# Router logits taken from rows that are not normalised yet, with mean and deviation applied to the logits of all tiles at once

## The chip, the cores and the metric

The kernel runs on one core of a Trainium2 chip. The metric is the device time of one execution in microseconds (us); less is better. Five engines work beside each other: TensorE (PE in the profile, with its weight loads as PEld), VectorE (DVE), ScalarE (ACT), GpSimd (POOL) and SyncE (SP), and 16 DMA engines move data for them.

## The reference, cut to what matters

The program is a whole network block followed by a second one of two layers. Each of these two layers is a mixer, a layer norm, and a mixture of 32 experts whose router reads the normalised rows:

```python
h = layer_norm(ALPHA * h + mixed, ln_g[i, 0], ln_b[i, 0])
ffn = hierarchical_moe(h, ...)
h = layer_norm(ALPHA * h + ffn, ln_g[i, 1], ln_b[i, 1])

def layer_norm(x, g, b):
    mu = mean(x); var = mean((x - mu)**2)
    return (x - mu) * rsqrt(var + LN_EPS) * g + b

def hierarchical_moe(h, w_group, b_group, w_expert, b_expert, ...):
    glog = xf @ w_group + b_group        # 4 groups
    elog = xf @ w_expert + b_expert      # 32 experts
    ...                                  # best group, top 2 experts in it, their gates
    ...                                  # each token's row goes through its 2 experts
```

So 36 logits per token (4 and 32) are wanted before any expert can start. Layer 0 has 514 rows here (2 rows of meta tokens and 512 tokens), layer 1 has 512.

## The kernel before, in words

Rows are tiled by 128 tokens: `xt[:, t, :]` holds tile t (128 x 1024, f32), and in layer 0 there is a small tile `hm` of 2 rows ahead of the four. In both layers `mix_ln` (L1812) closes the mixer: `token_mm` (L1496) multiplies the mixer's output by its last weight matrix, in two column halves. The second half is run tile by tile, so that the tiles end one after the other: 24 products of 512 columns each (8 blocks, three products of split operands), written to the bank `pz`.

When a tile's products end, a generator `steps` (L1832) is made for it. Its stages are: (1) `sum_` adds the product to the scaled row and takes the row's sum (DVE, L1830), and `ln_sums` (L1614) makes the negative mean `nm` (DVE) and the sum of squares (ACT, L1622); (2) `ln_norm` (L1626) makes 1/deviation by `rsq` (L345: a square root on ACT, then four small DVE operations and one for `nm`) and normalises the tile in place on ACT (L1629); (3) `xpose` (L2053) turns the tile with 8 PE transposes into two `prt` banks and copies them to `rht`, one half on DVE and one on ACT (L2061); (4) `ln_gain` (L1632) applies gain and bias on DVE and POOL together, for the last tile on DVE alone over all 1024 columns (L1638), and `keep` stores the tile to `dh` in DRAM from POOL's queue (L2041); (5) `route` (L2064) multiplies `rht` by the router's weights `wr` into the bank `plg` (8 products of 36 columns, each two passes in the profile) and adds the bias by a product of one row, `brt` (two passes).

The stages of neighbouring tiles are interleaved by hand in L1527 to L1536: after tile i's products come stage 1 of i, stage 3 of i-1, stage 2 of i, stage 4 of i-1 and stage 5 of i-2. What is left is run after the loop (L1848), and then `logits` (L2076) copies the logits from PSUM to `lg`. These blocks stand in `manual_schedule(engines=VA)`: the order of DVE's and ACT's instructions in such a block is the written one. PE's, POOL's and SP's order is a scheduler's, which takes instructions by the order in which they were written, as far as it holds them for ready.

`fold` (L2043), ahead of the products of `token_mm`, folds the layer norm's gain and bias into the router: `brt` gets bias x `wr` (8 products into `pbr`, an addition on DVE), and `wr` is multiplied by the gain (DVE). `moe` (L2085) starts from `lg`: the first instruction on it is the maximum `gm` (L2114), followed by a chain of small DVE operations, two PE groups (`prk`, `ptab`), a gather of rows (`xg`, POOL's queue) and the first expert's products (`peg`). The experts' weights are streamed from DRAM by SP into a ring of buffers, part of which are filled before `moe` starts.

Of the kernel before, what the change touches and what calls it, by code (L numbers as in the profile page):

```python
# [8 lines left out]
F32 = mybir.dt.float32  # L9
# [3 lines left out]
AF = mybir.ActivationFunctionType  # L13
OP = mybir.AluOpType
# [3 lines left out]
P = 128  # L18
S = 512
D = 1024  # L20
KT = D // P
NT = S // P
# [30 lines left out]
LN_EPS = 1e-5  # L53
# [9 lines left out]
VA = {mybir.EngineType.DVE, mybir.EngineType.Activation}  # L63
# [1432 lines left out]
def token_mm(e, nk, xx, done, tiles, before_tail=None, tail=8, steps=False):  # L1496

    left = deque()
    st = e.st
    for h in range(2):
        pz = [e.bank(f"pz{t}") for t in range(len(tiles))]

        def part(w, k, i):
            tk = tiles[i]
            e.mm3(pz[i][:tk.stop - tk.start], (xx[0][k][:, tk], xx[1][k][:, tk]), (w[0], w[1]), k == 0, k == nk - 1)

        k = 0
        while k < (nk if h == 0 else nk - tail):
            w = st.get()
            for i in range(len(tiles)):
                for j in range(w[0].shape[1]):
                    part([x[:, j, :] for x in w], k + j, i)
                if h == 0 and k + w[0].shape[1] == nk:
                    done(i, 0, pz[i])
            k += w[0].shape[1]
        if h == 1:  # L1520
            if before_tail:
                before_tail()
            ww = [st.get() for _ in range(tail // 2)]
            for i in range(len(tiles)):
                for j in range(tail):
                    part([x[:, j % 2, :] for x in ww[j // 2]], nk - tail + j, i)
                if steps:  # L1527
                    new = done(i, 1, pz[i])
                    last = list(left)[-1:]
                    with e.tc.manual_schedule(engines=VA):  # L1530
                        for g in [new] + last + [new] + last:
                            next(g)
                        if len(left) > 1:
                            next(left.popleft(), None)
                    left.append(new)
                    continue  # L1536
                if len(left) >= 2:
                    left.popleft()()
                left.append(done(i, 1, pz[i]))
    return left  # L1540
# [73 lines left out]
def ln_sums(e, pool, h, n, sums, junk, tag=""):  # L1614

    nm = pool.tile([P, 1], F32, name="lnm" + tag, bufs=4)[:n]
    ss = pool.tile([P, 1], F32, name="lns" + tag, bufs=4)[:n]
    if len(sums) == 2:
        e.ts(nm, sums[0], sums[1], -1.0 / D, OP.add, OP.mult)
    else:  # L1620
        e.ts(nm, sums[0], -1.0 / D)
    e.A.activation(junk, h, AF.Square, bias=nm, accum_out=ss)  # L1622
    return nm, ss


def ln_norm(e, pool, h, n, nm, ss, tag=""):  # L1626
    r = e.rsq(pool, ss, n, LN_EPS, "lnr" + tag)
    e.mul(nm, nm, r)
    e.A.activation(h, h, AF.Identity, scale=r, bias=nm)  # L1629


def ln_gain(e, h, n, g, b, c):  # L1632

    c = D - c
    for x, op in ((g, OP.mult), (b, OP.add)):
        if c < D:
            e.G.tensor_tensor(h[:, c:], h[:, c:], x[:n, c:], op=op)  # L1637
        e.V.tensor_tensor(h[:, :c], h[:, :c], x[:n, :c], op=op)  # L1638
# [173 lines left out]
def mix_ln(e, sp, zz, tiles, hs, mo):  # L1812


    e.st.limit = e.mark2 if mo.l else e.mark
    g = e.brow(sp, "ln_g_2", D, off=(mo.l * 2) * D, tag="lng0")
    b = e.brow(sp, "ln_b_2", D, off=(mo.l * 2) * D, tag="lnb0")
    sums = {}
    mo.fold()

    def done(i, h, p_):
        if h:
            return steps(i, p_)
        sum_(i, h, p_)

    def sum_(i, h, p_):
        n = tiles[i].stop - tiles[i].start
        c = slice(h * 512, h * 512 + 512)
        s_ = sums[i, h] = sp.tile([P, 1], F32, name=f"sum{i}{h}")[:n]
        e.V.scalar_tensor_tensor(hs[i][:, c], hs[i][:, c], ALPHA, p_[:n], op0=OP.mult, op1=OP.add, accum_out=s_)  # L1830

    def steps(i, p_):  # L1832
        sum_(i, 1, p_)
        n = tiles[i].stop - tiles[i].start
        nm, ss = ln_sums(e, sp, hs[i], n, [sums[i, 0], sums[i, 1]], sp.tile([P, D], BF, name="lnj")[:n])
        yield
        ln_norm(e, sp, hs[i], n, nm, ss)
        yield
        ht = mo.xpose(sp, hs[i], n)
        yield  # L1840
        t = i - (len(tiles) - NT)
        t = NT if t < 0 else t
        ln_gain(e, hs[i], n, g, b, 0 if i == len(tiles) - 1 else 448)
        mo.keep(t, hs[i], n)
        yield
        mo.route(ht, t, n)

    left = token_mm(e, KT, zz, done, tiles, steps=True)  # L1848
    with e.tc.manual_schedule(engines=VA):
        for gen in left:  # L1850
            for _ in gen:
                pass
        mo.logits()
# [41 lines left out]
def shortconv(e):  # L1895
# [62 lines left out]
    with tc.tile_pool(name="lo", bufs=1, reuse_waits="tile") as op:  # L1958
        mix_ln(e, op, z, [slice(t * P, (t + 1) * P) for t in range(NT)], [xt[:, t, :] for t in range(NT)], e.mo)
# [3 lines left out]
class Moe:  # L1963
# [76 lines left out]

        self.e.G.dma_start(self.dh[t * P:t * P + n, :], h)  # L2041

    def fold(self):  # L2043

        e = self.e
        pg, pb = [e.pc((n, 2 * D) if self.l else n, 0, KT) for n in ("ln_g_2", "ln_b_2")]
        pt = e.bank("pbr")[0:1, :36]
        for k in range(KT):
            e.mm(pt, pb[:, k:k + 1], self.wr[:, k, :], k == 0, k == KT - 1)
        e.add(self.br, self.br, pt)  # L2050
        e.mul(self.wr, self.wr, pg.unsqueeze(2).to_broadcast([P, KT, 36]))

    def xpose(self, pool, h, n):  # L2053

        e = self.e
        ht = pool.tile([P, KT, P], F32, name="rht", bufs=2)
        for k0 in (0, 4):
            pt = e.bank("prt")
            for k in range(4):
                e.tr(pt[:, k * P:k * P + n], h[:, (k0 + k) * P:(k0 + k + 1) * P])  # L2060
            (e.A.copy if k0 else e.V.tensor_copy)(ht[:, k0:k0 + 4, :n], pt.rearrange("p (k t) -> p k t", k=4)[:, :, :n])  # L2061
        return ht

    def route(self, ht, t, n):  # L2064

        e = self.e
        if self.pl is None:
            self.pl = e.bank("plg"), (e.bank("plg") if self.nt > NT else None)
        pl = self.pl[0][:, t * 36:(t + 1) * 36] if t < NT else self.pl[1][:n, :36]
        for k in range(KT):  # L2070
            e.mm(pl, ht[:, k, :n], self.wr[:, k, :], k == 0, False)
        e.mm(pl, self.one[:, :n], self.br[0:1, :], False, True)
        if t == NT:
            e.A.copy(self.lg[:n, t, :], pl)

    def logits(self):  # L2076

        self.done = self.e.A.copy(self.lg[:, :NT, :].rearrange("p t c -> p (t c)"), self.pl[0][:, :NT * 36])

    def run(self):  # L2080
        moe(self.e, self)
# [500 lines left out]
```

## Time and profile before

| | us |
|---|---|
| median of 3 runs (2554.54 to 2555.36) | 2554.92 |
| the profiled execution | 2554.61 |
| its span in the profile | 2552.8 |
| PE busy | 2300.2 (90%) |
| DVE busy | 944.4 (37%) |
| ACT busy | 666.8 (26%) |

The page's row of 40 slices shows PE at seven tenths or more nearly all the time; the DMA engines are nearly full in two stretches, slices 21 to 28 and 33 to 39, which are the experts of layer 0 and layer 1 (about 1278 to 1750 us and 2025 to 2510 us). Ahead of each stand the end of the mixer and the router. The busy time of an engine over the whole span says little about a change that sits in two stretches of some 90 us; the timelines of these stretches do. A row of a timeline has the start and the duration in us, engine, line, operation, what it writes and reads, the number of merged instructions, and in brackets the idle time before it with what ended it.

### The profile page before, as it was taken

The page shows a single profiled execution, that of the slowest core. Times are in us where ns is not written, and L with a number is a line of the kernel's source. Part 1 is how long each engine was busy: PE and PEld are TensorE (multiplying, and loading weights), DVE is VectorE, ACT ScalarE, POOL GpSimd, SP SyncE. Part 2 cuts the span into 40 slices and gives each one's busy share as a digit, 9 for nine tenths or more (in the row PEclk, how much of TensorE's full clock was granted, in tenths as well). Part 3 has the DMA queues.
Part 4 walks back from the last instruction along what each step waited for, and adds up shares of the span by engine and source line. Part 5 has one row for each costly group of instructions (what it writes and reads, how often), then busy time and mean ns, then how long its engine had stood idle before and what let it go on. Part 6 is the DMA issues. An engine that isn't in the chain of part 4 may idle for free. (4 is left out here: it accounts for less than half of the span.)

```text
span 2552.8 us, 37528 instructions
## 1 busy us (share of the span) xinstructions
PE 2300.2 (90%) x15343; PEld 1470.3 (58%) x15343; DVE 944.4 (37%) x2162; ACT 666.8 (26%) x1058; POOL 226.5 (9%) x264
## 2 busy tenths in 40 slices
PE   7998999999999999999799899884899798899881
PEld 6886777877888888887632233221798532233220
DVE  4348868765533332565620000003644610000003
ACT  4335432123422322375300000013322210000012
POOL 0023120000100000100200000001200210000002
PEclk9999999999999999999799999997899799999996
DMA  4221221025133242224589999998225599999993
GB/s 142 91 80 43 87 70 63 23 79 187 53 106 92 90 140 91 80 82 147 221 342 418 419 415 416 412 415 313 61 87 227 224 399 418 419 413 414 415 405 122
DMA packets 176434, 556.87 MB, mean 218 GB/s; under 512 B 22248, under 2 KB 104934, under 8 KB 127106
## 3 DMA queue, kind: packets, MB, share of 16 engines
q1 hardware_dynamic: 154308, 523.29, 53.0%
q0 software_dynamic: 12768, 25.31, 2.7%
q10 hardware_dynamic: 9184, 5.84, 0.8%
q8 instruction: 122, 2.00, 0.3%
q14 instruction: 52, 0.43, 0.1%
HBM read 548.02 MB, written 25.21 MB: 225 GB/s over the span
## 5 line engine op out<-in xcount | busy, mean ns | idle before, releaser
L300 PE MATMUL peg<-sr,ext 128*32 128x512 f32 (+1 forms) x4064 | 527.6, 599 | 70.9 <-DMA sr<-in_moe_w_gate_dram 38.7
L300 PEld LDWEIGHTS peg<-sr,ext 128*32 128x32 f32 (+1 forms) x4064 | 142.4, 111 | 410.8 <-issue 276.7
L300 PE MATMUL pey<-sr,eh 128*32 128x512 f32 x1984 | 303.3, 597 | 14.1 <-DMA sr<-in_moe_w_down_dram 11.8
L300 PEld LDWEIGHTS pey<-sr,eh 128*32 128x32 f32 x1984 | 82.0, 110 | 193.5 <-issue 148.6
L227 DVE TENSOR_TENSOR sh_0l<-sr,sh_0h 128x1024 fp32r<-128x1024 f32 x84 | 103.5, 1232 | 163.4 <-ACT sh_0h L225 162.8
L285 DVE TENSOR_TENSOR eh<-eh,peg 128x512 f32<-128x512 f32 x34 | 23.4, 688 | 367.4 <-PE peg L300 367.4
L2321 ACT COPY eys<-pey 128x512 f32<-128x512 f32 x68 | 39.9, 586 | 428.9 <-PE pey L300 428.4
L225 ACT CAST sh_0h<-sr 128x1024 fp32r<-128x1024 f32 x84 | 88.1, 1049 | 238.4 <-PE pf L300 53.2
L2264 DVE COPY ext<-pex 128x512 f32<-128x512 f32 x32 | 22.0, 689 | 311.1 <-PE pex L319 311.1
L227 DVE TENSOR_TENSOR sh_1l<-sr,sh_1h 128x1024 fp32r<-128x1024 f32 (+1 forms) x65 | 77.4, 1191 | 107.0 <-ACT sh_1h L225 106.7
L227 DVE TENSOR_TENSOR sh_2l<-sr,sh_2h 128x1024 fp32r<-128x1024 f32 (+1 forms) x65 | 74.2, 1141 | 94.5 <-ACT sh_2h L225 94.2
L225 ACT CAST sh_1h<-sr 128x1024 fp32r<-128x1024 f32 (+1 forms) x65 | 66.5, 1022 | 147.3 <-PE pf L300 48.5
L225 ACT CAST sh_2h<-sr 128x1024 fp32r<-128x1024 f32 (+1 forms) x65 | 62.9, 967 | 151.8 <-PE pf L300 49.3
L2290 ACT ACTIVATE eh<-peg 128x512 f32<-128x512 f32 x34 | 20.3, 597 | 278.0 <-PE peg L300 278.0
L300 PE MATMUL pl<-hlo,sh_0h 128*128 128x264 f32 (+3 forms) x288 | 87.5, 304 | 2.2 <-DVE hlo L309 2.2
L300 PE MATMUL pl<-hhi,sh_0h 128*128 128x264 f32 (+3 forms) x288 | 87.8, 305 | 0.8 <-ACT hhi L308 0.8
L300 PE MATMUL pl<-hhi,sh_0l 128*128 128x264 f32 (+3 forms) x288 | 87.0, 302 | 0.0
L2322 POOL DMA_INDIRECT dy<-eys,yix x34 | 33.9, 998 | 576.2 <-ACT eys L2321 559.8
L2300 DVE COPY eh<-pex 128x512 f32<-128x512 f32 x34 | 23.3, 691 | 136.0 <-PE pex L319 136.0
L2178 POOL DMA_INDIRECT xg<-dh,tix x34 | 35.4, 1041 | 326.3 <-PE pex L319 244.7
L2264 ACT COPY ext<-pex 128x512 f32<-128x512 f32 x36 | 21.1, 586 | 163.2 <-PE pex L319 118.7
L300 PEld LDWEIGHTS pl<-hlo,sh_0h 128*128 128x128 f32 x288 | 56.2, 195 | 5.0 <-DVE hlo L309 3.2
(747 smaller groups left out, 4898.2 us busy)
## 6 DMA issues: line engine op xcount, KB each, us to landing
sr<-in_moe_w_gate_dram SPq DMA_DIRECT2D x128, 1024.0 KB
sr<-in_moe_w_up_dram SPq DMA_DIRECT2D x122, 1024.0 KB
sr<-in_moe_w_down_dram SPq DMA_DIRECT2D x122, 1024.0 KB
sr<-in_w_in_dram SPq DMA_DIRECT2D x34, 1024.0 KB
sr<-in_sc_w_in_dram SPq DMA_DIRECT2D x12, 1024.0 KB
sr<-in_ffn_w_gate_dram SPq DMA_DIRECT2D x11, 1024.0 KB
sr<-in_ffn_w_up_dram SPq DMA_DIRECT2D x11, 1024.0 KB
sr<-in_ffn_w_down_dram SPq DMA_DIRECT2D x10, 1024.0 KB
```

The costliest lines, as they stand in the source:

```text
L225: self.e.A.copy(hi, r)
L227: v.tensor_tensor(lo, r, f(hi), op=OP.subtract)
L285: V.tensor_tensor(out_, a, b, op=OP.mult)
L300: T.matmul(o, l, r, start=start, stop=stop)
L2178: G.indirect_dma_start(out=xg[i], out_offset=None, in_=dh[:, :], in_offset=bass.IndirectOffsetOnAxis(ap=ti, axis=0), bounds_check=n_tok - ...
L2264: (A.copy if k0 or first else V.tensor_copy)(x_[:, k0:k0 + 4, :].rearrange("p k c -> p (k c)"), pt)
L2290: A.activation(sg, pg, AF.Silu)
L2300: V.tensor_copy(hh.rearrange("p k c -> p (k c)"), pt)
L2321: e.late = A.copy(ys[:, h * 512:(h + 1) * 512], po[h])
L2322: G.indirect_dma_start(out=dy[:, :], out_offset=bass.IndirectOffsetOnAxis(ap=yi, axis=0), in_=ys, in_offset=None, bounds_check=2 * n_tok - ...
```

## The change

`mean` and `deviation` are no longer applied to the rows ahead of the router. The turned tile holds the rows before normalisation, and the logits follow from L = r (x wr + nm c) + b, with c the column sums of the folded `wr` and b the folded bias. `fold` computes c for all 128 partitions by 8 products with a tile of ones, brings b to all partitions by one more product, and copies both to `cb`. `scales` keeps `nm` and r of each tile in `mr`. `route` loses the bias product, and for the 2-row tile its copy. `logits` does four DVE operations per group of tiles (the four full tiles; in layer 0 also the 2-row tile) in place of the ACT copy. The stages become three: (1) sums, r and the two copies to `mr`; (2) turning the tile, then normalising, gain, bias and store; (3) `route`. Stage 2 of a tile is issued in the middle of the next tile's products, stage 3 after them.

```diff
--- before.py
+++ after.py
@@ -1498,7 +1498,6 @@
 
 
 
-
     left = deque()
     st = e.st
     for h in range(2):
@@ -1524,15 +1523,15 @@
             for i in range(len(tiles)):
                 for j in range(tail):
                     part([x[:, j % 2, :] for x in ww[j // 2]], nk - tail + j, i)
+                    if steps and left and j == tail // 2 - 1:
+                        with e.tc.manual_schedule(engines=VA):
+                            next(left[0])
                 if steps:
-                    new = done(i, 1, pz[i])
-                    last = list(left)[-1:]
+                    left.append(done(i, 1, pz[i]))
                     with e.tc.manual_schedule(engines=VA):
-                        for g in [new] + last + [new] + last:
-                            next(g)
+                        next(left[-1])
                         if len(left) > 1:
                             next(left.popleft(), None)
-                    left.append(new)
                     continue
                 if len(left) >= 2:
                     left.popleft()()
@@ -1816,7 +1815,7 @@
     g = e.brow(sp, "ln_g_2", D, off=(mo.l * 2) * D, tag="lng0")
     b = e.brow(sp, "ln_b_2", D, off=(mo.l * 2) * D, tag="lnb0")
     sums = {}
-    mo.fold()
+    mo.fold(sp)
 
     def done(i, h, p_):
         if h:
@@ -1832,14 +1831,15 @@
     def steps(i, p_):
         sum_(i, 1, p_)
         n = tiles[i].stop - tiles[i].start
+        t = i - (len(tiles) - NT)
+        t = NT if t < 0 else t
         nm, ss = ln_sums(e, sp, hs[i], n, [sums[i, 0], sums[i, 1]], sp.tile([P, D], BF, name="lnj")[:n])
-        yield
-        ln_norm(e, sp, hs[i], n, nm, ss)
+        r = e.rsq(sp, ss, n, LN_EPS, "lnr")
+        mo.scales(t, n, nm, r)
         yield
         ht = mo.xpose(sp, hs[i], n)
-        yield
-        t = i - (len(tiles) - NT)
-        t = NT if t < 0 else t
+        e.mul(nm, nm, r)
+        e.A.activation(hs[i], hs[i], AF.Identity, scale=r, bias=nm)
         ln_gain(e, hs[i], n, g, b, 0 if i == len(tiles) - 1 else 448)
         mo.keep(t, hs[i], n)
         yield
@@ -2040,15 +2040,29 @@
 
         self.e.G.dma_start(self.dh[t * P:t * P + n, :], h)
 
-    def fold(self):
+    def fold(self, pool):
 
         e = self.e
+        ones, self.cb, self.mr = [pool.tile([P] + sh, F32, name=n) for n, sh in
+                                  (("rone", [P]), ("rcb", [72]), ("rmr", [2, self.nt]))]
+        e.V.memset(ones, 1.0)
         pg, pb = [e.pc((n, 2 * D) if self.l else n, 0, KT) for n in ("ln_g_2", "ln_b_2")]
-        pt = e.bank("pbr")[0:1, :36]
+        pt = e.bank("pbr")
         for k in range(KT):
-            e.mm(pt, pb[:, k:k + 1], self.wr[:, k, :], k == 0, k == KT - 1)
-        e.add(self.br, self.br, pt)
+            e.mm(pt[0:1, :36], pb[:, k:k + 1], self.wr[:, k, :], k == 0, k == KT - 1)
+        e.add(self.br, self.br, pt[0:1, :36])
         e.mul(self.wr, self.wr, pg.unsqueeze(2).to_broadcast([P, KT, 36]))
+
+        pt = e.bank("pbr")
+        for k in range(KT):
+            e.mm(pt[:, :36], ones, self.wr[:, k, :], k == 0, k == KT - 1)
+        e.mm(pt[:, 36:72], self.one, self.br, True, True)
+        e.V.tensor_copy(self.cb, pt[:, :72])
+
+    def scales(self, t, n, nm, r):
+
+        self.e.V.tensor_copy(self.mr[:n, 0, t:t + 1], nm)
+        self.e.V.tensor_copy(self.mr[:n, 1, t:t + 1], r)
 
     def xpose(self, pool, h, n):
 
@@ -2068,14 +2082,21 @@
             self.pl = e.bank("plg"), (e.bank("plg") if self.nt > NT else None)
         pl = self.pl[0][:, t * 36:(t + 1) * 36] if t < NT else self.pl[1][:n, :36]
         for k in range(KT):
-            e.mm(pl, ht[:, k, :n], self.wr[:, k, :], k == 0, False)
-        e.mm(pl, self.one[:, :n], self.br[0:1, :], False, True)
-        if t == NT:
-            e.A.copy(self.lg[:n, t, :], pl)
+            e.mm(pl, ht[:, k, :n], self.wr[:, k, :], k == 0, k == KT - 1)
 
     def logits(self):
 
-        self.done = self.e.A.copy(self.lg[:, :NT, :].rearrange("p t c -> p (t c)"), self.pl[0][:, :NT * 36])
+        e = self.e
+        for t0, t1, n, pl in ((0, NT, P, self.pl[0]), (NT, self.nt, 2, self.pl[1])):
+            if t0 < t1:
+                sh = [n, t1 - t0, 36]
+                lg = self.lg[:n, t0:t1, :]
+                of = lambda k: self.mr[:n, k, t0:t1].unsqueeze(2).to_broadcast(sh)
+                row = lambda k: self.cb[:n, k * 36:(k + 1) * 36].unsqueeze(1).to_broadcast(sh)
+                e.V.tensor_tensor(lg, row(0), of(0), op=OP.mult)
+                e.add(lg, lg, pl[:n, :(t1 - t0) * 36].rearrange("p (t c) -> p t c", c=36))
+                e.V.tensor_tensor(lg, lg, of(1), op=OP.mult)
+                e.V.tensor_tensor(lg, lg, row(1), op=OP.add)
 
     def run(self):
         moe(self.e, self)
```

## Rows read from the trace of the kernel before

**Rows 1.** Busy time by stretch: stretch, length, engines with instruction counts, PE clock, DMA share, GB/s

```profile
1184.00:1245.50 61.50, 61.50 (x303) 45.12 (x301) 29.89 (x72) 23.27 (x35) 8.63 (x9) 1.00 0.51 197
1268.00:1272.00 4.00, 1.73 (x9) 1.65 (x8) 3.36 (x6) 0.00 (x0) 0.00 (x0) 0.50 0.00 0
1944.00:1992.80 48.80, 48.80 (x244) 40.49 (x244) 20.28 (x50) 14.86 (x20) 5.81 (x6) 1.00 0.60 228
```

**Rows 2.** Timeline of PE, layer 1, between the third and the fourth tile

```profile
1984.16 1.03 PE L319 MATMUL prt<-ident,xt 128*128 128x128 f32 x8
1985.03 1.87 PE L300 MATMUL plg<-wr,rht 128*128 128x36 f32 x16
1986.84 0.41 PE L300 MATMUL plg<-brt,stage 1*128 1x36 f32 x2
1987.17 0.50 PE L300 MATMUL pz<-sh_0h,zh 128*128 128x512 f32 x1
1987.51 0.40 PE L300 MATMUL pz<-sh_0l,zh 128*128 128x512 f32 x1
```

**Rows 3.** Timeline of PE, layer 1, after the last tile's products

```profile
1992.78 1.04 PE L319 MATMUL prt<-ident,xt 128*128 128x128 f32 x8
1993.65 1.87 PE L300 MATMUL plg<-wr,rht 128*128 128x36 f32 x16
...
1998.23 1.97 PE L319 MATMUL prt<-ident,xt 128*128 128x128 f32 x8
2000.13 3.63 PE L300 MATMUL plg<-wr,rht 128*128 128x36 f32 x16
```

**Rows 4.** Timeline of DVE, layer 1, from the last tile's sum to the router

```profile
1992.98 0.69 DVE L1830 SCALAR_TENSOR_TENSOR xt<-xt,pz 128x512 f32<-128x512 f32 x1 [3.22 <-PE pz L300]
...
1996.82 0.75 DVE L1638 TENSOR_TENSOR xt<-xt,lng 128x576 f32<-128x576 f32 x1
...
1999.38 0.69 DVE L2061 COPY rht<-prt 128x512 f32<-128x512 f32 x1 [1.02 <-PE prt L319]
2000.31 1.23 DVE L1638 TENSOR_TENSOR xt<-xt,lng 128x1024 f32<-128x1024 f32 x1 [0.23 <-PE prt L319]
2004.75 0.17 DVE L2114 TENSOR_REDUCE gm<-lg 128x4 f32<-128x16 f32 x1 [1.96 <-ACT lg L2078]
```

**Rows 5.** Timeline of ACT, layer 1, the last tile's normalisation

```profile
1996.94 1.24 ACT L1629 ACTIVATE xt<-xt,lnm,lnrr 128x1024 f32<-128x1024 f32 x1 [1.07 <-DVE lnm L285]
```

**Rows 6.** Timeline of DVE, layer 0, the 2-row tile from its sum to r

```profile
1217.66 0.68 DVE L1830 SCALAR_TENSOR_TENSOR hm<-hm,pz 2x512 f32<-2x512 f32 x1 [3.23 <-PE pz L300]
...
1220.82 0.15 DVE L285 TENSOR_TENSOR lnrr<-lnrr,lnrt 2x1 f32<-2x1 f32 x1
```

**Rows 7.** Timeline of DVE, layer 1, one operation of the router and the next

```profile
2006.32 0.29 DVE L285 TENSOR_TENSOR sel<-lg,ge 128x128 f32<-128x128 f32 x1
2006.65 0.38 DVE L2130 TENSOR_REDUCE el<-sel 128x32 f32<-128x128 f32 x1
```

**Rows 8.** Timeline of PE and of DVE, layer 0: last products' end, router's start

```profile
1245.53 1.03 PE L319 MATMUL prt<-ident,xt 128*128 128x128 f32 x8
...
1257.51 0.18 DVE L2114 TENSOR_REDUCE gm<-lg 128x5 f32<-128x20 f32 x1 [1.94 <-ACT lg L2078]
```

**Rows 9.** Timeline of all engines around `fold`, layer 0

```profile
1183.10 0.62 ACT L1771 ACTIVATE lm<-lav 128x528 f32<-128x528 f32 x1
...
1183.40 0.68 PE L300 MATMUL pbr<-wr,par 128*1 128x36 f32 x16
...
1184.12 0.18 DVE L288 TENSOR_TENSOR brt<-brt,pbr 1x36 f32<-1x36 f32 x1 [1.75 <-PE pbr L300]
1184.22 0.44 DVE L285 TENSOR_TENSOR wr<-wr,par 128x288 f32<-128x288 f32 x1
...
1184.60 0.69 DVE L297 SCALAR_TENSOR_TENSOR lm<-lm,ltg 128x528 f32<-128x528 f32 x1
```

**Rows 10.** Timeline of ACT, layer 0, the loads into the pool of `mix_ln`

```profile
1195.87 0.37 ACTq L397 DMA_DIRECT2D lng<-in_ln_g_dram  x1
```

## The prediction

> **What bounds the kernel now.** I read the 40 slices of the page first, then busy time by stretch, then the timelines of PE, DVE and ACT in the two stretches that the change touches, and last the timeline of all engines around `fold`. The page's chain of waits covers only the end of the execution, so it says nothing here. From the start of the last mixer product to the end of it PE is busy without a gap, 61.5 of 61.5 us in layer 0 and 48.8 of 48.8 us in layer 1, at the full clock of 2.4 GHz [rows 1]. Any PE instruction added there moves the end of the products by its own pace. After the products, PE's part ends and a chain of one tile decides: sum, r, normalise (ACT), turn (PE), copy, logits (PE), copy, `gm`. From the end of the last products to `gm` it is 2004.75 - 1992.78 = 11.97 us in layer 1 and 1257.51 - 1245.53 = 11.98 us in layer 0 [rows 3, 4, 8]. The DMA engines have by then filled all the buffers they may: in layer 0 they move 0 GB/s just before the experts begin, and the page's slices show them full from then to the end of the experts. So the experts' stream starts when the router lets it, and a microsecond won or lost before `gm` is one at the end, in each layer. What is to be worked out is therefore where `gm` starts in each layer.
>
> **Prices.** PE at full clock, from start to start [rows 2]: 8 transposes 1985.03 - 1984.16 = 0.87; the 16 passes of one tile's logits 1.81; the bias product 0.33; and the first dense product after such a group takes 0.34 instead of 0.23 (the other 23 of the tile need 1992.78 - 1987.51 = 5.27), so each return costs 0.11 [rows 2, 3]. On DVE an operation on 128 x 128 elements is followed by a dependent one after 0.33 [rows 7], and one on 1 x 36 elements takes 0.18 [rows 9].
>
> **Part 1, `fold`.** It adds 8 products of 36 columns with a full 128 x 128 weight tile, the form of one tile's logits (1.81), one product with a single row (0.33), and one return (0.11): 2.25 us of PE per layer. The products need the scaled `wr`, which DVE ends at 1184.66 [rows 9], when PE is already in its dense stretch; there is no gap that could hide them [rows 1]. So 2.25 is on the path; the upper end is 0.7 more, if PE meets them right behind `pbr` and waits for `wr`, the lower end is 1.1, if the 16 passes cost no more than the 16 of `pbr`, 0.68 [rows 9], which have the same 36 columns but a weight tile of one column. I take 2.25, since the trace has the very form in the logits. The memset of ones and the copy to `cb` are one small DVE operation each beside PE's work, where DVE is busy 29.9 of 61.5 us [rows 1]; were they late, only the products of `fold` would feel it (rival 3).
>
> **Part 2, the order on PE.** Before, the turn of tile 2, the logits of tile 1 and, behind them, those of tile 2 ran after the last dense product, under the chain of the last tile, whose own turn begins at 1998.23 [rows 3]: hidden. Now the turn of tile 2 stands in the middle of the last tile's products, and the logits of tile 1 stand ahead of them. Only the logits of tile 2 are left for the shelter. So the last product ends later by 0.87 + 1.81. Three more returns cost 0.33, one bias product (that of tile 0) is gone, -0.33: 2.68 in layer 1. In layer 0 there is the 2-row tile too: four more returns, two bias products gone of which the small one is about 0.2: 0.87 + 1.81 + 0.44 - 0.53 = 2.59. With `fold` the products end 4.93 us later in layer 1 and 4.84 in layer 0. The SP queue's loads into the split buffers wait for these products and slide along, but they end several us before they are wanted [rows 1].
>
> **Part 3, the chain of the last tile.** Let E be the end of its products on PE. The sum starts at E + 0.2 if DVE is free [rows 3, 4]. It isn't: tile 2's turn ends about E - 2.8 (half a tile's products and a return later PE is at E); then come the copies of `rht` (0.69 on DVE, about 0.6 on ACT), the normalisation on ACT (1.24, to E - 0.8) and gain and bias on DVE, 2 x 0.79, and all of this is written ahead of the last tile's sum. So the sum starts at about E + 0.7. If it could pass them it would be E + 0.2; that is the lower end. From the sum to r it is 1220.97 - 1217.66 = 3.3 in a tile where nothing stands between [rows 6]: E + 4.0. Then in DVE's order: the two copies to `mr` 0.25; the copy of `rht` 0.65 (the turn, freed at E + 1.8 by the logits of tile 2, is long done); `nm` x r 0.17; ACT's normalisation 1.24 and 0.12 for the two hand-overs [rows 5]; gain and bias over all 1024 columns, 2.45 [rows 4]; and only then the four operations of `logits` on 144 elements, 4 x 0.32 [rows 7]. `gm` starts at E + 0.7 + 3.3 + 0.25 + 0.65 + 0.17 + 1.36 + 2.45 + 1.28 = E + 10.2. Layer 0 has four more operations on the 2-row tile, 4 x 0.2: E + 11.0. PE doesn't bind: its last 16 passes start when `rht` is copied, E + 4.9, and at the low clock of 1.2 GHz, at which the trace shows them (3.6 [rows 3]), end at E + 8.6, before DVE asks for them at E + 9.2. What the change saves here is the normalisation and the turn ahead of the logits; what it puts in their place is the same normalisation, with gain and bias, ahead of the four operations, because they stand in one DVE queue.
>
> That a DVE instruction holds up what is behind it shows once in the trace: the addition to `brt` waits 1.75 us for PE, and the next-but-one instruction, whose input from ACT was there at 1183.72, starts at 1184.60 [rows 9]. The Trainium skill says the same more broadly (TensorE: Matmul & The Clock Gate, on the architecture of the array): the queues of ScalarE and VectorE are strictly first in, first out, and only TensorE's may pull weight loads forward. That rule speaks against this change as it is written; without it rival 1 would be the likelier, at 2553.7 instead of 2561.7 for the execution, and the one wait in the trace agrees with the rule.
>
> **Sum.** Layer 1: 4.93 + 10.2 - 11.97 = +3.2. Layer 0: 4.84 + 11.0 - 11.98 = +3.9. Together +7.1 on the profiled execution of 2554.61 us; the median of the runs is 0.3 higher, so I say 2562.0. With the lower ends (sum not held up, `fold` at 1.1) it is 7.1 - 1.0 - 2.3 = +3.8; with the upper one of `fold` +8.5. POOL's store of the last tile slides with gain and bias to about E + 9, its memsets behind it to E + 12; the gather follows `gm` by 13 us and more (it did in the trace of before) and doesn't see it.
>
> **Rivals.**
> 1. The change does what it says: DVE takes the copy of `rht` while ACT squares, and the four operations don't stand behind the normalisation. Then `rht` is there at E + 3.3, the logits at full clock end at E + 5.1, r at E + 3.5, and `gm` starts at E + 6.2 (layer 0: 7.0). Layer 1: 4.93 + 6.2 - 11.97 = -0.8; layer 0: 4.84 + 7.0 - 11.98 = -0.1. That is 2554.0 on the median's scale: not slower. Even so it gains next to nothing, since the shelter of part 2 is paid for. For it speaks that the data would allow it; against it the written order of DVE and ACT. It decides if DVE's operations of the last tile appear out of the written order.
> 2. The same chain, but shorter on one side: the scheduler lets the last tile's sum pass tile 2's gain and bias (they stand in different blocks), or leaves the turn of tile 2 behind the last products. Some 1 to 4 us less than the forecast: +3 to +5, 2558 to 2560.
> 3. `fold` stalls PE. The tile of ones lies in a pool whose first loads are only issued at 1195.87 in layer 0, when the memory of the stage before is given up [rows 10]. If PE's order has the products of `fold` early, at 1184, PE waits up to 11 us there, and the time is 2566 to 2573. Against it: in the trace DVE waited for PE at `fold` and not PE for DVE [rows 9], so PE is rather late against the order it was given.
> 4. A gain of over 5 us: needs the products of `fold` and the turn of tile 2 both off the path, for which I see no place.
>
> **How the numbers follow.** The forecast (+5 to +10) has 0.52, rival 1 0.16 (-3 to +2), rival 2 0.18, rival 3 0.08, rival 4 0.06. What a measurement of this kernel can tell from no change is about 0.2%, 5.1 us. The edge of that bound, 2560.0, lies at the foot of the forecast's range, so a part of it (0.04) counts as no change: slower 0.48 + 0.08 = 0.56; same 0.16 + 0.18 + 0.04 = 0.38; faster 0.06. The range from 2553.5 to 2567 leaves out rival 4, the low half of rival 1 and most of rival 3.
>
> **What would show it.** In the profile of the changed kernel: 16 passes of `wr` with ones and two of one row, some 2.2 us of PE, near 1184 and 1944, without an idle PE; the last `pz` group of layer 1 ending near 1997.7 and of layer 0 near 1250.4; tile 2's turn in the middle of the last group; the last tile's sum on DVE right behind the second `lnb` operation of tile 2; the 1024-column gain and bias ahead of the four operations; `gm` near 1261.4 in layer 0 and, shifted by layer 0's 3.9, near 2011.8 in layer 1; the experts' stretches as long as before. It is wrong if the four operations come ahead of the gain, if the dense stretches end less than 4 us later, or if a stretch of the experts changes its length by more than the two stretches before it.

## The result, and the profile after

The changed kernel is slower: 2583.21 us (median of 4 runs, 2581.49 to 2585.37) against 2554.73 us (2554.34 to 2555.36) for the kernel before, a ratio of 1.0112 with a 95% interval of 1.0098 to 1.0127. That is 28.5 us more, where 7.1 had been forecast, and outside the range of 2553.5 to 2567. The span of the profiled execution is 2579.8 us against 2552.8. `gm` starts 20.55 us later in layer 0 (1278.06) and 27.76 later in layer 1 (2032.51) [rows 4, 8]. So some 20 us are lost ahead of `gm` of layer 0 and some 7 more ahead of that of layer 1; from there to the end nothing is lost (547.3 us against 548.0).

The first view is busy time by stretch of the changed kernel (columns as in [rows 1]; the first and third stretch hold `fold`, the others the dense products behind it).

```profile
1182.60:1201.00 18.40, 5.13 (x37) 4.62 (x36) 8.95 (x15) 8.34 (x13) 0.00 (x0) 0.64 0.30 96
1201.00:1266.20 65.20, 65.20 (x322) 48.06 (x320) 25.80 (x71) 17.03 (x24) 12.41 (x10) 0.97 0.44 168
1963.80:1969.50 5.70, 3.09 (x36) 2.79 (x35) 3.04 (x6) 1.56 (x2) 0.00 (x0) 0.98 0.87 309
1969.50:2021.30 51.80, 51.80 (x250) 43.34 (x250) 21.04 (x55) 14.10 (x19) 8.55 (x7) 0.97 0.51 185
```

PE, which had no gap in [rows 1], is busy for 5.13 of 18.40 us and for 3.09 of 5.70 us. Its timeline says what it waited for (such a time in which PE is idle is called a stand below); layer 0 around `fold`, then layer 1:

```profile
1182.66 0.68 PE L300 MATMUL pbr<-wr,par 128*1 128x36 f32 x16
1196.61 3.60 PE L300 MATMUL pbr<-wr,rone 128*128 128x36 f32 x16 [13.27 <-DVE rone L2048]
...
1200.71 0.59 PE L300 MATMUL pz<-sh_0h,zh 128*2 128x512 f32 x1
...
1204.08 0.63 PE L300 MATMUL pz<-sh_0h,zl 128*128 128x512 f32 x1
1204.51 0.49 PE L300 MATMUL pz<-sh_0h,zh 128*128 128x512 f32 x1
```

```profile
1963.87 0.68 PE L300 MATMUL pbr<-wr,par 128*1 128x36 f32 x16
1967.16 1.95 PE L300 MATMUL pbr<-wr,rone 128*128 128x36 f32 x16 [2.61 <-DVE rone L2048]
...
1969.40 0.79 PE L300 MATMUL pz<-sh_0h,zh 128*128 128x512 f32 x1
1970.00 0.63 PE L300 MATMUL pz<-sh_0l,zh 128*128 128x512 f32 x1
```

Before each group of 16 passes with `rone`, the tile of ones, PE stands for 13.27 and 2.61 us until DVE's memset of it is done. Afterwards it runs at half pace: dense products follow each other by 0.43 us instead of 0.23, from 1200.71 to 1204.8 in layer 0 and from 1969.40 to 1972.8 in layer 1. The granted clock is 0.51 in both stretches (the level of 1.2 GHz) and 1.00 (2.4 GHz) right behind them. DVE shows the other side, layer 0, then layer 1:

```profile
1193.66 1.27 DVE L285 TENSOR_TENSOR lgx<-lm,yb 128x514 f32<-128x514 f32 x2
1195.02 1.30 DVE L309 TENSOR_TENSOR zl<-lgx,zh 128x514 fp32r<-128x514 f32 x2
1196.30 0.17 DVE L2048 MEMSET rone<- 128x128 f32 x1
```

```profile
1965.07 1.21 DVE L227 TENSOR_TENSOR sh_0l<-sr,sh_0h 128x1024 fp32r<-128x1024 f32 x1
1966.20 0.67 DVE L309 TENSOR_TENSOR zl<-szc,zh 128x512 fp32r<-128x512 f32 x1
1966.85 0.17 DVE L2048 MEMSET rone<- 128x128 f32 x1
```

The memset is 0.17 us long, and it stands behind the last operations of the mixer. The program's own tile addresses say why it can't be earlier in layer 0: `rone` occupies bytes 81280 to 81792 of each partition, and the two buffers of `yb` of the stage before 77184 to 81408 and 81408 to 85632, so that it overlaps both; the last reading of `yb`, from the second, is the first line above, over at 1194.93. In layer 1 (80544 to 81056) the memory is free by 1917.7, as e2 below shows in its trace; there the memset only stands behind the operations of the mixer that are queued ahead of it, the last two of which take from 1965.07 to 1966.85.

The tail of layer 1 on DVE, and the same time on POOL:

```profile
2020.43 0.76 DVE L1637 TENSOR_TENSOR xt<-xt,lng 128x576 f32<-128x576 f32 x1 [1.44 <-ACT xt L1842]
2021.23 1.58 DVE L1637 TENSOR_TENSOR xt<-xt,lnb 128x576 f32<-128x576 f32 x1
2022.73 0.67 DVE L1829 SCALAR_TENSOR_TENSOR xt<-xt,pz 128x512 f32<-128x512 f32 x1
...
2028.61 1.22 DVE L1637 TENSOR_TENSOR xt<-xt,lng 128x1024 f32<-128x1024 f32 x1 [1.31 <-ACT xt L1842]
2029.87 1.22 DVE L1637 TENSOR_TENSOR xt<-xt,lnb 128x1024 f32<-128x1024 f32 x1
2031.01 0.30 DVE L2096 TENSOR_TENSOR lg<-rcb,rmr 128x144 f32<-128x144 f32 x1
...
2032.51 0.17 DVE L2135 TENSOR_REDUCE gm<-lg 128x4 f32<-128x16 f32 x1
...
2032.65 1.28 DVE L2393 CAST eh<-pid 128x128 f32<-128x128 int32 x1
2032.79 1.15 DVE L2137 TENSOR_TENSOR ge<-lg,gm 128x16 f32<-128x16 f32 x1
```

```profile
2020.48 1.70 POOL L1636 TENSOR_TENSOR xt<-xt,lng 128x448 f32<-128x448 f32 x1 [3.95 <-ACT xt L1842]
2022.26 1.54 POOL L1636 TENSOR_TENSOR xt<-xt,lnb 128x448 f32<-128x448 f32 x1
...
2031.93 1.86 POOL L2122 MEMSET xg<- 128x1024 f32 x2
```

The order is the one forecast: the last tile's sum right behind tile 2's second `lnb` operation, and the 1024-column gain and bias ahead of the four operations that make the logits. Two durations are not: the second operation of tile 2 takes 1.58 us, and the first operations behind `gm` 1.15 to 1.28.

### The profile page after: what moved, and what is told of

Same layout as the page of the kernel before. It is cut to its first block, busy times and chain, and to the rows that moved or that the text cites. A ratio compares the mean times of both kernels' runs of the same rounds, so it can differ in the third digit from the quotient of the medians.

```text
span 2579.8 us, 37602 instructions
## 1 busy us (share of the span) xinstructions
PE 2297.9 (89%) x15361; PEld 1468.4 (57%) x15361; DVE 954.2 (37%) x2196; ACT 666.0 (26%) x1055; POOL 232.9 (9%) x264
```

## The experiments

Each kernel is timed beside the kernel before on its own chip (2554.25 to 2554.76 us). To see past the differences of a few us with which the stretches begin, the table takes two lengths from each profile: A, from the start of `pbr` at `fold` to the start of the last dense product, and B, from there to `gm`. e2, e3, e9 and e11 have their numbers in their own parts.

| kernel | median, us | ratio to before (95%) | A, layers 0 / 1 | B, layers 0 / 1 | A + B of both, against before |
|---|---|---|---|---|---|
| before | 2554.3 to 2554.8 | | 61.90 / 48.47 | 12.21 / 12.20 | |
| after | 2583.21 | 1.0112 (1.0098 to 1.0127) | 83.22 / 57.13 | 12.18 / 11.51 | +29.3 |
| e1, ones early | 2563.52 | 1.0036 (1.0021 to 1.0050) | 66.97 / 53.70 | 12.18 / 11.52 | +9.6 |
| e5, e1 and logits first | 2562.43 | 1.0031 (1.0020 to 1.0041) | 66.97 / 53.72 | 12.01 / 11.32 | +9.2 |
| e7, e1 and turns as before | 2564.27 | 1.0033 (1.0021 to 1.0046) | 64.29 / 51.03 | 15.72 / 14.55 | +10.8 |
| e4, cheap fold | 2561.75 | 1.0025 (1.0015 to 1.0035) | 65.09 / 51.80 | 12.18 / 11.52 | +5.8 |
| e8, e4 and normalising beside logits | 2555.87 | 1.0005 (0.9996 to 1.0015) | 65.09 / 51.81 | 10.34 / 9.75 | +2.2 |
| e10, e8 and two operations | 2554.96 | 1.0000 (0.9990 to 1.0009) | 65.08 / 51.82 | 9.97 / 9.41 | +1.5 |
| e12, e10, gain on POOL, memory moved | 2555.91 | 1.0006 (0.9997 to 1.0015) | 65.09 / 51.82 | 7.30 / 6.23 | -4.3 |

**e1: the ones made early.** They go into a constant of the router, written when each layer begins (1065.7 and 1808.6) and refilled with its own numbers after `fold`.

```diff
-        G.iota(const("slot", [P]), pattern=[[1, P]], ...)
+        V.memset(const("slot", [P]), 1.0)
...
-        e.V.memset(ones, 1.0)
+        ones = self.slot
...
         e.V.tensor_copy(self.cb, pt[:, :72])
+        e.G.iota(ones, pattern=[[1, P]], ...)
```

> The changed kernel, but the tile of ones is not set in fold: it is the router's own constant tile, filled with ones when the layer begins and given its final content after fold; all of the 18 products of fold stay, and only what they wait for is gone. Theory (PE stands at fold because the memset of ones runs late on VectorE, 13.3 us in layer 0 and 2.6 us in layer 1, and the dense products after the pause run their first microseconds at 1.2 GHz): the two stalls and most of the slow products go, 2583.2 - 21 = 2562, between 2560 and 2564. Rival (the loss sits in the new order on PE and in the last tile's chain): no change, 2581 to 2584.

Measured 2563.52 us: 19.7 of the 28.5 us are gone. PE at `fold` in layer 0:

```profile
1183.45 0.68 PE L300 MATMUL pbr<-wr,par 128*1 128x36 f32 x16
1184.87 1.95 PE L300 MATMUL pbr<-wr,slot 128*128 128x36 f32 x16 [0.73 <-ACT ltg L1764]
...
1187.08 0.39 PE L300 MATMUL pz<-sh_0h,zh 128*2 128x512 f32 x1
```

The stand is 0.73 us and no slow stretch follows (granted clock 1.00 from 1187.08 on). The row names ACT for it; the scaled `wr`, which the passes read, is done at 1184.72, and layer 1 of e2 names it. By the table A loses 16.25 us in layer 0 and 3.43 in layer 1, 19.7 as the medians say. Of the 16.25, 14.4 are the longer stretch from `pbr` to the first dense product (18.05 against 3.63); the rest is the lower clock behind it.

**e2: the memset on GpSimd** (`e.G.memset(ones, 1.0)`), which takes it out of DVE's queue and leaves it in its memory.

> The changed kernel, but the memset of ones is issued on GpSimd, into the same tile at the same place. If the memset is late because of what stands ahead of it in VectorE's queue, GpSimd does it at once and the time is that of the run with the ones set early, about 2562. If it is late because its memory is still held by the stage before, the pause in layer 0 stays (11 to 13 us) and the one of layer 1 goes or not with its memory: 2575 to 2583.

Measured 2577.39 us, ratio 1.0093 (1.0076 to 1.0110). The timeline of PE, layer 0, then layer 1:

```profile
1196.80 3.63 PE L300 MATMUL pbr<-wr,rone 128*128 128x36 f32 x16 [11.98 <-POOL rone L2048]
...
1963.91 1.95 PE L300 MATMUL pbr<-wr,rone 128*128 128x36 f32 x16 [0.73 <-DVE wr L285]
```

DVE and POOL in layer 0:

```profile
1195.16 1.27 DVE L285 TENSOR_TENSOR lgx<-lm,yb 128x514 f32<-128x514 f32 x2
1196.54 0.21 POOL L2048 MEMSET rone<- 128x128 f32 x1 [131.56 <-ACT zh L308]
```

Layer 0 keeps a stand of 11.98 us, with POOL idle ahead of the memset: it waits for the memory, and starts at 1196.54, right behind the last reading of `yb`, over at 1196.43. (The row names ACT for the wait; the program has the memset wait for that reading.) A of layer 0 is 81.43 us, 1.79 less than in the changed kernel. In layer 1 the memset starts at 1917.7, early, and only the 0.73 us of `wr` remain: there it was the place in DVE's queue.

**e3: the added part of `fold` alone**, in the kernel before; nobody reads what it makes.

```diff
+        ones, self.cb, self.mr = [pool.tile([P] + sh, F32, name=n) for n, sh in ...]
+        e.V.memset(ones, 1.0)
...
+        for k in range(KT):
+            e.mm(pt[:, :36], ones, self.wr[:, k, :], k == 0, k == KT - 1)
+        e.mm(pt[:, 36:72], self.one, self.br, True, True)
+        e.V.tensor_copy(self.cb, pt[:, :72])
```

> The kernel before with only the added part of fold (the tile of ones, the 9 products, the copy), whose results nobody reads; logits, stages and order are those of before. Theory: fold alone carries most of the loss: 2 x 2.25 us for the products and 21 for the pauses and the clock after them, 2554.7 + 25.5 = 2580, between 2576 and 2584. Rival (the loss sits in the order and the chain): only the products' own 4.5, 2559.

Measured 2580.24 us, ratio 1.0099 (1.0082 to 1.0116); PE stands 13.27 us ahead of the products again. `fold` alone costs 25.9 us (against 2554.33), nearly all of the 28.5.

**e5: the last tile's logits written ahead of its normalisation, gain and store**, on top of e1.

```diff
         ht = mo.xpose(sp, hs[i], n)
+        if i == len(tiles) - 1:
+            mo.route(ht, t, n)
+            yield
         e.mul(nm, nm, r)
...
-        for gen in left:
-            for _ in gen:
-                pass
+        next(left[0])
         mo.logits()
+        for _ in left[0]:
+            pass
```

> The run with the ones set early, and for the last tile of a layer the logits written ahead of its normalisation, gain, bias and store. Theory (in VectorE's queue the normalisation, 1.2 us on ScalarE with its hand-overs, and 2.5 us of gain and bias stand between r and the four operations): 3.9 us less per layer than with the ones set early alone, 2562 - 7.8 = 2554, that is, about as fast as the kernel before. Rival (something else, as PE's last products, holds the logits): less than 2 us in all, 2560 or more.

Measured 2562.43 us, not 2554. The logits did come first, and `gm` didn't follow them. DVE in layer 1:

```profile
2011.49 0.31 DVE L2103 TENSOR_TENSOR lg<-lg,rcb 128x144 f32<-128x144 f32 x1
...
2013.18 1.23 DVE L1637 TENSOR_TENSOR xt<-xt,lng 128x1024 f32<-128x1024 f32 x1 [1.31 <-ACT xt L1845]
2014.44 1.23 DVE L1637 TENSOR_TENSOR xt<-xt,lnb 128x1024 f32<-128x1024 f32 x1
2015.58 0.16 DVE L2139 TENSOR_REDUCE gm<-lg 128x4 f32<-128x16 f32 x1
```

The wait for ACT's normalisation and the two gains only changed places with the four operations: `gm`, the router's first instruction, still has them ahead of it in DVE's queue.

**e7: the turns as before**, the turn of a tile after the next tile's products and its logits one tile later, on top of e1.

```diff
-                    if steps and left and j == tail // 2 - 1:
-                        with e.tc.manual_schedule(engines=VA):
-                            next(left[0])
                 if steps:
+                    last = list(left)[-1:]
                     left.append(done(i, 1, pz[i]))
                     with e.tc.manual_schedule(engines=VA):
-                        next(left[-1])
-                        if len(left) > 1:
+                        for x in [left[-1]] + last:
+                            next(x)
+                        if len(left) > 2:
                             next(left.popleft(), None)
```

> The changed kernel with the ones taken early (2563.5), but the tiles' turns and logits again interleaved as before the change: the turn of the next-to-last tile after the last tile's products, its logits after that, instead of both ahead of the last products. Theory that PE's order sets the end of the stage (Part 2 of the prediction): the last products end 2.6 to 2.7 us earlier in each layer, 2558. Rival that VectorE's chain from the last sum to gm sets it: the earlier end of the products only puts the copies of two turns and the gain of the tile before between the last sum and gm, and the time stays at 2562 to 2564; gm then comes 2 to 3 us later after the end of the last products than the 11 to 12 us of the changed kernel.

Both halves can be read. The dense products do end earlier by 2.68 us in each layer (A), the 0.87 + 1.81 of the prediction's part 2. B grows by 3.54 and 3.03, since the turn, normalisation and gain of tile 2 then stand between the last sum and `gm`. 2564.27 us: nothing is won, and the chain on DVE decides.

**e4: column sums with a weight of one column.** In `fold` the raw `wr` is multiplied by the gain column instead of the scaled `wr` by ones, and one product with a row of ones spreads the result after the first tile's first half.

```diff
-        e.V.memset(ones, 1.0)
...
-            e.mm(pt[0:1, :36], pb[:, k:k + 1], self.wr[:, k, :], k == 0, k == KT - 1)
+        for c, x in ((0, pg), (36, pb)):
+            for k in range(KT):
+                e.mm(pt[0:1, c:c + 36], x[:, k:k + 1], self.wr[:, k, :], k == 0, k == KT - 1)
...
-            e.mm(pt[:, :36], ones, self.wr[:, k, :], k == 0, k == KT - 1)
+    def spread(self):
+        pt = self.e.bank("pbr")
+        self.e.mm(pt[:, :72], self.one, self.rw, True, True)
```

> The column sums that fold needs are taken with the gain column as a weight of one column (16 passes, like the 16 of the added bias) instead of with a 128x128 tile of ones, and are spread over the partitions by one small product after the last products of the first tile. No tile of ones, so no wait of PE for it. Theory (what is left after the pause is the sum of the prediction, of which fold is 2.25 us of PE per layer): 16 products of 128*1 cost 0.68 us a layer where the 16 of 128*128 cost 1.95, so 1.2 to 1.3 us a layer less than in the kernel with the ones taken early (2563.5): about 2561. Rival (the rest of the loss lies in the last tile's chain on VectorE alone, and PE's products at fold are covered): no change, 2563.5. Rival (the slower clock after a short stand costs more than the products): PE's idle time of 0.7 us at fold stays and the time is 2563 to 2564.

Measured 2561.75 us. A falls by 1.88 and 1.90 us, more than the 1.2 to 1.3 expected, since the stand of 0.73 us for `wr` is gone too:

```profile
1184.73 1.20 PE L300 MATMUL pbr<-wr,par 128*1 128x36 f32 x32
1185.86 0.39 PE L300 MATMUL pz<-sh_0h,zh 128*2 128x512 f32 x1
```

**e8: the last tile in one block**, on top of e4: its turn's copies behind the square, its logits ahead of gain and store, so that ACT normalises while DVE makes the logits.

```diff
+        end = i == len(tiles) - 1
+        if end:
+            ht = mo.xpose(sp, hs[i], n)
         r = e.rsq(sp, ss, n, LN_EPS, "lnr")
...
         e.A.activation(hs[i], hs[i], AF.Identity, scale=r, bias=nm)
+        if end:
+            mo.route(ht, t, n)
+            mo.logits()
         ln_gain(e, hs[i], n, g, b, 0 if i == len(tiles) - 1 else 448)
```

> The kernel with the cheap fold, and the last tile written as one block: its turn's copies behind the square, its logits ahead of normalising, gain and keeping, so that ScalarE's normalising stands beside VectorE's four logits operations and the two 1.25 us gains stand behind gm. Theory (VectorE's chain from the last sum to gm sets the end): gm comes 2 x 1.25 us earlier after the end of the last products in each layer, about 2556 if all of it comes through. Rival (gm is written behind the gains in VectorE's queue whatever this block says, as with the logits alone put first): no gain over the cheap fold, about 2561.

Measured 2555.87 us, the 2556 of the theory, but by another sum than the one on record: `gm` still starts behind both gains. DVE in layer 1:

```profile
2003.88 0.31 DVE L2110 TENSOR_TENSOR lg<-lg,rcb 128x144 f32<-128x144 f32 x1
2004.18 1.23 DVE L1638 TENSOR_TENSOR xt<-xt,lng 128x1024 f32<-128x1024 f32 x1
2005.44 1.23 DVE L1638 TENSOR_TENSOR xt<-xt,lnb 128x1024 f32<-128x1024 f32 x1
2006.58 0.16 DVE L2146 TENSOR_REDUCE gm<-lg 128x4 f32<-128x16 f32 x1
...
2006.72 0.22 DVE L2404 CAST eh<-pid 128x128 f32<-128x128 int32 x1
```

B is 1.84 and 1.77 us shorter: the gains start without a wait for ACT, which normalised beside the four operations. Behind `gm` another microsecond comes in layer 1: the cast takes 0.22 us instead of 1.28, since POOL's memset of `xg` is no longer running beside it (it starts at 2007.50). From `gm` to the gather it is 12.85 us in layer 1 instead of 13.84, but 14.92 instead of 14.33 in layer 0, where the memset now runs beside a later operation, which takes 1.35 us (1260.29). Together that is 4.0 us of the 5.9; the rest isn't located (the stretch starts 1.4 us earlier in this profile, and such starts differ by up to 3.4 us between the runs).

**e10: two operations per tile for the logits**, with mean and deviation as scalars of each partition, in place of four over all tiles and the copies to `mr`.

```diff
+        e.stt(lg, self.cb[:n, :36], nm, pl, OP.mult, OP.add)
+        e.stt(lg, lg, r, self.cb[:n, 36:], OP.mult, OP.add)
```

> The last kernel, with the logits of each tile made by two operations with a per-partition scalar each (column sum times mean plus product; that times deviation plus bias) as soon as its products are there, in place of four operations over all tiles and two copies of mean and deviation per tile. The four operations of 0.30 us and two copies of 0.1 us on the chain become two of about 0.15 us for the last tile: 1 us per layer less than the run with normalising beside the logits. If that run gives 2556: about 2554; if it gives 2561: about 2559. Rival (scheduled order puts the gains ahead all the same, and PE's order is the bound): within 0.5 us of that run.

Measured 2554.96 us against 2554.76 for the kernel before: the same. The step is worth 0.35 us per layer in B, not 1, because the gains then wait 0.81 us for ACT.

**e9: gain and bias of every tile on DVE alone**, on top of e1 (`ln_gain(e, hs[i], n, g, b, 0)`).

> The changed kernel with the ones taken early (2563.5), but gain and bias of every tile on VectorE alone (1024 columns) instead of split into 576 on VectorE and 448 on GpSimd. Theory (GpSimd's and VectorE's two-input operations exclude each other while both run, so the split buys no time): the pair 0.76 + 1.58 = 2.34 us of the split tiles becomes 2 x 1.23 = 2.46 us, the last sum starts within 0.2 us of where it did after the last products, and the time stays at 2563.5 +- 1. Rival (VectorE's second operation takes 1.58 us because its operand comes late or the memory is busy, not because of GpSimd): then 1024 columns take over 2 us each and the last sum comes 2 us or more later in each layer, 2567 or more.

Measured 2563.36 us, ratio 1.0031 (1.0019 to 1.0042), e1's time. The same tile of layer 1 on DVE:

```profile
2003.97 1.23 DVE L1637 TENSOR_TENSOR xt<-xt,lng 128x1024 f32<-128x1024 f32 x1 [1.31 <-ACT xt L1842]
...
2005.72 1.22 DVE L1637 TENSOR_TENSOR xt<-xt,lnb 128x1024 f32<-128x1024 f32 x1
```

All 1024 columns take 1.23 + 1.22 = 2.45 us, where 576 took 0.76 + 1.58 = 2.34 beside POOL. Splitting the tile buys 0.1 us.

**e11 and e12: the last tile's gain on GpSimd**, on top of e10, in four operations of 512 columns; e12 also takes the router's two large tiles first, so that its small ones land in other memory.

```diff
+            for x, op in ((g, OP.mult), (b, OP.add)):
+                for c in (0, 512):
+                    y = hs[i][:, c:c + 512]
+                    e.G.tensor_tensor(y, y, x[:n, c:c + 512], op=op)
...
-        G.memset(oh[:, nt, :], 0.0)
+        V.memset(oh[:, nt, :], 0.0)
...
+        for i in range(2):                                      # e12 alone
+            sp.tile([P, KT, P], F32, name="ext", bufs=2)
```

> The kernel with two operations for the logits of a tile (2555.0), and gain and bias of the last tile on GpSimd alone, in four operations of 512 columns, so that VectorE's queue holds nothing between the last logits and gm (a memset of 0.14 us for the router goes from GpSimd to VectorE). Theory (the two gains of 1.23 us stand ahead of gm only by their place in VectorE's queue; nothing of the router needs them before the gather 12 us later): gm comes 3.1 us earlier after the last products in each layer, less what GpSimd takes from VectorE's operations while both run: about 2550, between 2549 (nothing taken) and 2552 (1.3 us taken in each layer). Rival (GpSimd's four operations, about 1.3 us each alone, hold VectorE's small operations up one after the other, as one operation was held up for 1.2 us behind GpSimd's memset): 2555 or more. Rival (the kept rows land too late for the gather): gm earlier by 3 us, gather not, 2555.

> The kernel with the last tile's gain on GpSimd (2559.6), with the router's two large tiles taken first from the memory that the stage gives up, so that gm and the router's other small tiles no longer lie in the memory of the gain row that GpSimd's multiplications still read (addresses 72352 to 76448 in layer 1; gm was at 73376, now at 81568, which the last square gave up before). Theory (gm waited 3.37 us for that memory, as the tile of ones waited for the memory of another): gm starts right behind the last logits, 3.4 us earlier after the last products than in that kernel, less about 1 us for each VectorE operation that stands behind one of GpSimd's four: 2554 to 2557. Rival (gm waits for GpSimd by its place in a queue or because both engines share their way to memory, whatever its address): gm waits 3 us again and the time stays at 2559 to 2560.

e11 measured 2559.63 us (1.0018, 1.0009 to 1.0028), slower than e10 and not the 2550 of the theory. DVE and POOL, layer 1 of e11:

```profile
2008.91 0.17 DVE L2142 TENSOR_REDUCE gm<-lg 128x4 f32<-128x16 f32 x1 [3.37 <-POOL xt L1857]
```

```profile
2006.40 2.48 POOL L1857 TENSOR_TENSOR xt<-xt,lng 128x512 f32<-128x512 f32 x2 [3.32 <-ACT xt L1849]
```

`gm` starts when POOL's second multiplication by the gain row ends (2008.88). By the program's addresses `gm` lay inside that row, `lng` (72352 to 76448; `gm` at 73376), here as in the kernel before: no form of the router could have started ahead of the last multiplication by gain. With `gm` at 81568 (e12) it starts right behind the last logits (2003.66, 0.26 us), and what comes next shows, on DVE and then on POOL:

```profile
2003.95 0.17 DVE L2144 TENSOR_REDUCE gm<-lg 128x4 f32<-128x16 f32 x1
...
2004.81 1.26 DVE L2150 TENSOR_TENSOR ge<-iom,gf 128x16 f32<-128x16 f32 x1
2006.11 1.30 DVE L285 TENSOR_TENSOR sel<-lg,ge 128x128 f32<-128x128 f32 x1
```

```profile
2004.78 2.48 POOL L1857 TENSOR_TENSOR xt<-xt,lng 128x512 f32<-128x512 f32 x2 [3.34 <-DVE lst L2404]
```

B is 2.7 and 3.2 us shorter than in e10, but the gather follows `gm` by 17.7 and 16.7 us instead of 14.9 and 12.9: while POOL multiplies (from 2004.78), operations of DVE that took 0.18 and 0.29 us in e8 take 1.26 and 1.30. 2555.91 us, no gain. None of the kernels beats the one before.

## Why the prediction was wrong, point by point

**Part 1, the memset: the step that failed.** "The memset of ones and the copy to `cb` are one small DVE operation each beside PE's work" holds for the copy and not for the memset. Were they late, "only the products of `fold` would feel it", the prediction goes on; but the dense products stand behind them on PE, and those that start at 1187.08 in e1 waited until 1200.71. So not the length of the memset counts but the time at which it can run, and that is set by its memory and its place in DVE's queue. e1, e2 and e3 show it: 16.25 us in layer 0, of which e2 gives back the 1.79 of DVE's queue and the memory holds the rest, and 3.4 us in layer 1, the queue alone. That the change makes the kernel slower came true, but 19.7 of the 28.5 us come from a term that the sum put at nothing.

**Rival 3** named the mechanism and the row: the pool's memory comes free near 1195.87 [rows 10], and the memset ran at 1196.30. It was priced too low (11 us for a stand of 13.27, nothing for the slower clock behind it, nothing in layer 1) and put at 0.08 by a misread row. "DVE waited for PE at `fold` and not PE for DVE" [rows 9] is about the addition to `brt`, which reads `pbr`; it says nothing of an operation whose memory is still in use. The row that bore on it was [rows 10].

**Part 1, the price of the products.** From `pbr` to the first dense product it is 3.63 us in e1 against 0.61 before: 3.0, not 2.25. It is the upper end of the prediction, with its reason: PE meets the products behind `pbr` and waits 0.73 for `wr`. The price behind the lower end, a weight of one column, is what e4 measures: 1.13 us for 32 passes, 0.5 more than the 16 of before (its spreading product, later, comes on top).

**Part 2** holds in its main term: e7 against e1 gives 2.68 us per layer, 0.87 + 1.81, though with the returns, put at 0.44 and 0.33 more, it would have been 3.1 and 3.0. So A grows by 5.07 and 5.23 in e1 where 4.84 and 4.93 were forecast: `fold` cost 0.8 more per layer and the order on PE 0.5 less. That the two partly cancel is luck.

**Part 3** has the right order and lacks a microsecond per layer. From the end of the last products `gm` comes after 11.94 and 11.28 us (forecast 11.0 and 10.2). Most of it is one term: gain and bias of tile 2 were put at 2 x 0.79, and the second takes 1.58, so the sum starts 1.5 us after the end of the products and not 0.7. In the kernel before, the split halves of tile 2 didn't fall into the same time; POOL was through with its half before DVE's first operation at 1996.82 [rows 4]:

```profile
1993.97 1.13 POOL L1637 TENSOR_TENSOR xt<-xt,lng 128x448 f32<-128x448 f32 x1 [3.06 <-PE prt L319]
1995.18 1.13 POOL L1637 TENSOR_TENSOR xt<-xt,lnb 128x448 f32<-128x448 f32 x1
```

The change brought them together.

**The sum without the stand** was 7.1 us; e1 measures 9.2 (2563.52 against 2554.33), and 9.6 by A and B of its profile. The 2.5 us from 7.1 to 9.6 are the terms above: 0.5 in A and, to the end of B, 0.9 and 1.1.

**Rival 1** is refuted as the trace of after has it, and e5 adds the reason that the prediction only half had: the four operations ahead of the gain would not have helped, since `gm` itself stands behind it, in the queue and in memory. **The first-in-first-out rule** of the Trainium skill (TensorE: Matmul & The Clock Gate, on the architecture of the array) agrees with the orders shown here: in e5 `gm` starts at 2015.58, behind the gains, though the last logits are done at 2011.80. It doesn't decide alone there, since the address of `gm` asks for the same. **Rival 2** (2558 to 2560) and **rival 4** didn't happen. The experts' stretches kept their lengths, as forecast.

## What to carry to other kernels

A new tile that an in-order engine needs early must be costed by when its memory is free and what is ahead of its writer, not by the length of the writer: look up which tile had the bytes before it and when that was last read. Where a change takes an operation off a chain, ask what the next instruction on the chain waits for besides its data; here `gm` stood behind the gain by queue and by address, so freeing its data won nothing. Work moved ahead of the last dense products is paid on TensorE (2.68 us per layer here), and a small form of it (a weight of one column, 1.9 us per layer less in e4) is worth having.

## What the runs showed of the hardware that I had not expected

GpSimd's and VectorE's operations with two inputs in SBUF didn't run at once here. Alone, GpSimd's 448 columns take 1.13 us (1993.97 in the kernel before), VectorE's 576 take 0.75 [rows 4] and its 1024 take 1.23; together GpSimd's 448 take 1.70 and 1.54, and VectorE's 576 up to 1.58. The last tile's sum, whose second input lies in PSUM, kept its 0.67 us beside GpSimd (2022.73), and a reduction with one input in e12 kept the 0.38 us that it takes in e8 (`el`, 2007.44). A cast with one input didn't keep its time beside GpSimd's memset: 1.28 us instead of 0.22 (e8). The Trainium skill (SBUF — State Buffer, "SBUF: two separate sides") describes an exclusive lock on a shared pair of ports, held for a whole instruction; the stretches of 1.26 and 1.30 us in e12 beside GpSimd's operations of 1.24 agree.

TensorE's clock fell to 1.2 GHz after a stand of 2.61 us too, and not at once: the 16 passes behind it ran at full pace (1.95 us, granted clock 1.00), and the slow products (0.51) began 2.2 us after the stand had ended. After the 0.73 us of e1 it didn't fall.
